# Attention and GLA decoder layer on one core: scalings with an accumulator, the inputs' low part one unit later, gate splits behind exponentials and copies, and the first rows squared first at the joint

## The chip, the cores and the metric

The kernel runs on one core of a Trainium2 chip. Its engines are called here as in the profile: PE (TensorE, products and transposes), DVE (VectorE), ACT (ScalarE), POOL (GpSimd) and SP (SyncE, which here only starts transfers). Each engine works through its own queue in order; semaphores make one wait for another. The time is device microseconds for one execution, lower being better. Three runs of the kernel before took 2201.93, 2202.55 and 2204.05 us.

## The reference

One layer of a decoder whose heads are split in two groups, on 2048 prompt tokens and 8 x 8 sample tokens. The core of it:

```python
def hybrid_layer(x, pos, ...):
    h = rms_norm(x, g_mix_pre)
    proj = jnp.einsum('btd,de->bte', h, w_in)
    q, k, v, gq, gk, gv, gr, glr = jnp.split(proj, points, axis=-1)
    q, k = rope(q), rope(k)
    attn = swa_banded(q, k, v, sinks)            # window of 128, 8 heads, 2 kv heads, sinks
    log_a = log_sigmoid(glr @ w_gk2 + b_gk) / 16
    o, s_new = gla_chunked(gq, gk, gv, log_a, s0)    # 4 heads, gated linear attention
    o = rms_norm(o, g_gla) * silu(gr)
    x = x + rms_norm(concat(attn, o) @ w_out, g_mix_post)
    h = rms_norm(x, g_ffn_pre)
    u = relu(h @ w_up)
    return x + rms_norm((u * u) @ w_down, g_ffn_post), ...

def sink_softmax(scores, mask, sink):
    m = max(max(scores), sink)
    p = exp(scores - m)
    return p / (sum(p) + exp(sink - m))
```

All of it is fp32. The model's width is 1024, the inner width of the MLP 4096. The keys, values and states that go to the next step are outputs too.

## The kernel before

**Numbers.** Products on PE take operands in a rounded form (fp32r). So most operands are split into a high part (ACT copies and rounds) and a low part (DVE subtracts the high part from the source), and a product is made of three: high-high, high-low and low-high. In names, h and l end the two parts: xh, xl for the transposed inputs, ph, pl for the transposed probabilities, qh, ql, kh, kl for queries and keys. The gate's weights wg are split in the same way, after a multiply by the gain of the norm (gcol).

**Attention stage** (about 30 to 305 us). The prompt is cut into 16 blocks of 128 tokens. For each block i the loop runs four units u = 0 to 3, one for two heads each. A unit (function `unit`) is a generator of steps: scores sc on PE; mask and maximum on DVE (a custom reduction that writes s and m); exponentials on ACT, with their sum den; reciprocal and scaling of s by it (line 501 on DVE, 499 on ACT for one of eight scalings in half of the units); transposes pT on PE; ph on ACT; pl on DVE; products av on PE, first ph with the values, then pl; and the sum mo. Three units are in work at a time (ahead, now, behind). Around their steps the loop puts the work for other blocks: projections of block i + 2 fill PE, and a table, `A_PLAN`, says in which unit and phase (T, A, X, S, B, C in this order) each piece of the rest is issued: x0 and x1, the low parts of the two halves of the transposed inputs of block i + 3; klo and lo, low parts of keys and queries; rstd, the norm's power on POOL. The queues follow this order of issue.

Every result of PE goes to a bank of PSUM. The kinds d and e, with the transposed inputs xT and the av products, have one buffer each, the others two.

From block 3 on, two pieces of the gate's weights are fetched per block (16 pieces of 128 x 384 in the stage, 192 KB each, into two buffers). `split_gw` multiplies a piece by gcol on POOL (line 261), copies the high part on ACT and subtracts on POOL (263). `A_SPLIT` says that two pieces are split at phase B of unit 0. The first two pieces are split in block 4. `split_gained` (221) does the same work for later pieces without the multiply: ACT copies with a scale, and DVE multiplies and subtracts in one instruction.

SP starts the loads and stores, in order: the pieces' loads, the stores of mixed rows, and the stores of each block's transposed inputs (xt_d, 512 KB for each part).

**GLA stage** (about 300 to 700 us). For each block, level products are put into one matrix AH by predicated copies (`put_level`), copied to AT, and the state S is updated (1179); then PE makes o. The sample's output goes through `finish_out` with i == NB, in the midst of a prompt block's work: norm over each head (squares on ACT, power on POOL giving ors), then four scalings on DVE (1088), and after two pauses of 44 products their transposes on PE.

**Joint** (about 700 to 890 us). Output projections of 128 rows each, `out_projecting`, in the order `B_ORDER`. While one set of rows is projected, `residual` works on earlier ones: norm, residual sum, second norm, scaling by its gain (1515), transposes to PE (xnT, 1525), and splits. The first rows come with their sum made already; of them only the second norm is left. The second rows are the ones called bx.

Of the kernel before, what the change touches and what calls it, by code (L numbers as in the profile page):

```python
# [16 lines left out]
ALU = mybir.AluOpType  # L17
# [4 lines left out]
P = 128  # L22
# [3 lines left out]
NB = T // P  # L26
# [27 lines left out]
H_EARLY, H_LATE = (1, 2), (5, 7, 6, 3, 4)  # L54
G_EARLY, G_LATE = (0, 1), (2, 3)
A_FILL = ((11, 2, 0), (10, 0, 2), (10, 0, 0), (12, 1, 0))
A_LEAD, A_SPLIT = 14, (2, 1, 0, 0)
A_PLAN = [(name, (int(at[0]), at[1])) for name, at in dict(
    klo0="3T", first="1B", hi1="3C", x1="1B", lo1="0A", klo1="0B", x0="0C", rest="3A", lo0="3A", junk="2A", turn="1A", rstd="1A", vl="3S"
).items()]  # L60
G_FIRST = (0, 1)
G_NEXT = (NB, *range(2, NB))
G_ORDER = (0, 1, 2, 3)
G_FILL = (34, 14, 16, 8, 20)
# [76 lines left out]
def hybrid_step_kernel(ctx: ExitStack, tc: tile.TileContext, I, O):  # L141
# [113 lines left out]
        return c, k, load_raw(sp, k, G_AT + c * G_N, G_N, f"wg{c}", *stage)  # L255

    def split_gw(c, k, raw):
        if c in G_LATE:
            split_gained(gw[c][1][:, k, :], gw[c][2][:, k, :], raw, k)
            return  # L260
        nc.gpsimd.tensor_tensor(raw, raw, gcol[:, k : k + 1].to_broadcast([P, G_N]), op=ALU.mult)
        ac.activation(gw[c][1][:, k, :], raw, AF.Copy)
        nc.gpsimd.tensor_tensor(gw[c][2][:, k, :], raw, f32(gw[c][1][:, k, :]), op=ALU.subtract)
# [201 lines left out]
    def unit(i, r, jj, mo):  # L465
# [31 lines left out]
        for u in range(2):  # L497
            if u == 0 and r == jj:
                ac.activation(s[:, u, :nk], s[:, u, :nk], AF.Copy, scale=den[:, u : u + 1])
            else:  # L500
                dv.tensor_scalar(s[:, u, :nk], s[:, u, :nk], den[:, u : u + 1], None, op0=ALU.mult)
        yield
        pT = bank([P, nkt, 2, P], "c", f"pT_{u_}")
        for u in range(2):
# [289 lines left out]
    for i in range(NB):  # L794
# [29 lines left out]

        def do(u, phase):
            for name, at in A_PLAN:
                if at == (u, phase) and name in todo:
                    todo.pop(name)()

        for u in range(4):  # L830
            next(now)
            do(u, "T")
            next(behind, None)
            next(now)
            do(u, "A")
            later = next(queue)
            next(later)
            run(fill, A_FILL[u][0])
            next(behind, None)
            if u != 3:  # L840
                next(behind, None)
            run(fill, A_FILL[u][1])
            if u == 0:
                next(now)
            if u < 2 and new:
                hi, todo[f"x{u}"] = x_half(i + 3, u)
                hi()
            elif u == 2:
                todo.update(heads_T(i + 1))
            do(u, "X")  # L850
            run(fill, A_FILL[u][2])
            if u:
                next(now)
            do(u, "S")
            if u == 3:
                next(behind, None)
            next(behind, None)
            next(ahead)
            next(now)
            do(u, "B")  # L860
            split_some(A_SPLIT[u] if i < NB - 1 else 1)
            next(now)
            do(u, "C")
            behind, now, ahead = now, ahead, later
# [210 lines left out]
    def finish_out(i, og_src, sg, n, kind):  # L1075
# [9 lines left out]
            yield 44, True  # L1085
        og = next(ogs) if i < NB else gp_s[:, :512].rearrange("p (h d) -> p h d", h=4)
        for h in range(4):
            nc.vector.scalar_tensor_tensor(
                og[:n, h, :], og_src(h), rs[:n, h : h + 1], sg[:n, h * P : (h + 1) * P],
                op0=ALU.mult, op1=ALU.mult,  # L1090
            )
        for _ in range(S_WAIT[0] if i == NB else 1):
            yield 44, True
        pt = bank([P, 4, P], kind, f"ogT_{i}")
# [519 lines left out]
    for n, i in enumerate(B_ORDER[2:]):  # L1614
# [1 line left out]
        mixing = out_projecting(nc.tensor, i, early[-1][1])  # L1616
        run(mixing, 24 if i == B_ORDER[-1] else 48)
        if n == 0:
            second = residual(*early.pop(1))
            next(second)  # L1620
            next(second)
        elif n == 1:
            run(second)
        if i == B_ORDER[-1]:
            waiting_rows = residual(*early.pop(0))
            run(waiting_rows, 5)
        elif n != 1:
            run(residual(*early.pop(0)))
        run(mixing)
        if n == len(B_ORDER) - 5:  # L1630
# [614 lines left out]
```

## Time and profile before

| | |
|---|---|
| median of three runs | 2202.55 us (2201.93 to 2204.05) |
| the profiled execution | 2200.13 us |
| span of its trace, first to last instruction | 2198.2 us |
| mean granted clock of TensorE | 0.997 |
| attention stage, 36.7 to 300 us: PE / DVE / ACT / POOL busy | 255.98 / 227.65 / 223.00 / 152.64 us |
| GLA, 300 to 700 us: PE / DVE / ACT busy | 396.4 / 299.0 / 250.5 us |
| joint, 700 to 890 us: PE / DVE / ACT busy | 188.32 / 120.31 / 82.89 us |
| MLP, 890 to 2198 us: PE / DVE / ACT busy | 1290.11 / 866.61 / 643.28 us |

Busy times are those of the trace's windows. In a row of the timeline the first number is the start and the second the duration, in us; the words behind name engine, line, operation, what is written and read, and the shape; "x2" joins equal instructions in a row. In square brackets stands how long the engine sat idle before, and who released it. DVE's and ACT's rows overlap their neighbours at both ends, so the step from one start to the next is shorter than a duration. Most of the small instructions carry line 130, that of a helper that records them; they are told apart by the names of their tiles.

### The profile page before, as it was taken

The numbers are of one execution on the slowest core, as the hardware profiler recorded it, in microseconds if no ns is written. First come the engines' busy times: TensorE is split into PE (matmuls) and PEld (weight loads), VectorE is DVE, ScalarE is ACT, GpSimd is POOL, SyncE is SP. The second block draws the span as 40 slices with busy tenths as digits, with TensorE's granted clock in tenths as the row PEclk, the third lists the DMA queues.
The fourth block names the chain that finished last, engine by engine and source line by source line (L and its number), as shares of the span: only waits on it lengthen the run. The fifth ranks groups of instructions, "written<-read, shape, count | busy, mean of one in ns | idle before, by whom it ended". The sixth has DMA issues, their size and how long they took to land.

```text
span 2198.2 us, 34114 instructions
## 1 busy us (share of the span) xinstructions
PE 2158.6 (98%) x11784; PEld 1861.8 (85%) x11784; DVE 1532.1 (70%) x3101; ACT 1220.7 (56%) x2626; POOL 261.8 (12%) x418
## 2 busy tenths in 40 slices
PE   8999999999999999899999999999999999999998
PEld 7989989999998888788888887888888888888886
DVE  5888868777786665888888655548676666555566
ACT  5889867556664443555555544435454544444454
POOL 3576512121211100000000000000000000000000
PEclk9999999999999999999999999999999999999999
DMA  7344232214436765868777676758554433766685
GB/s 229 131 137 157 97 103 73 68 63 145 142 126 230 224 204 185 277 219 278 269 254 260 236 237 220 241 181 268 182 187 158 138 138 146 239 201 193 195 271 185
DMA packets 240314, 411.53 MB, mean 187 GB/s; under 512 B 25925, under 2 KB 142125, under 8 KB 236029
## 3 DMA queue, kind: packets, MB, share of 16 engines
q1 hardware_dynamic: 240140, 409.35, 56.1%
q8 instruction: 93, 1.52, 0.3%
q14 instruction: 81, 0.66, 0.1%
HBM read 265.82 MB, written 143.99 MB: 186 GB/s over the span
## 4 chain that ended last, share of the span: by engine, by line
PE 85%; DVE 6%; ACT 4%; DMA 3%; issue 1%; POOL 1%; SPq 0%; DVEq 0%; ACTq 0%; POOLq 0%
PE dn L130 26%; PE gproj L130 10%; PE uc L130 8%; PE uX L130 7%; PE out L1318 6%; PE proj L130 5%; PE ue L130 4%; PE ud L130 4%; PE ub L130 4%; PE sam L130 1%; PE dsam L130 1%; PE av L130 1%; PE o L130 1%; PE pT L130 1%; PE sc L130 1%
## 5 line engine op out<-in xcount | busy, mean ns | idle before, releaser
L130 PE MATMUL dn<-o0t,o0s 128*128 128x512 f32 x896 | 349.2, 390 | 2.5 <-ACT f L2013 1.6
L130 PE MATMUL dn<-o1t,o0s 128*128 128x512 f32 x896 | 349.5, 390 | 0.5 <-DVE o1t L219 0.4
L130 PE MATMUL dn<-o0t,o1s 128*128 128x512 f32 x896 | 349.3, 390 | 0.0
L219 DVE TENSOR_TENSOR o1s<-rs,o0s 128x512 fp32r<-128x512 f32 x224 | 154.8, 692 | 229.8 <-ACT o0s L218 226.1
L218 ACT ACTIVATE o0s<-rs 128x512 fp32r<-128x512 f32 x224 | 141.1, 631 | 305.9 <-PE dn L130 286.8
L130 PE MATMUL gproj<-wg,gxh 128*128 128x384 f32 x1024 | 272.5, 342 | 0.3 <-DVE gp_s L213 0.3
L130 PEld LDWEIGHTS dn<-o0t,o0s 128*128 128x128 f32 x896 | 168.2, 188 | 39.5 <-ACT f L2013 2.0
L130 PEld LDWEIGHTS dn<-o1t,o0s 128*128 128x128 f32 x896 | 168.2, 188 | 37.6 <-DVE o1t L219 1.6
L130 PEld LDWEIGHTS dn<-o0t,o1s 128*128 128x128 f32 x896 | 168.2, 188 | 35.4
L130 ACT ACTIVATE st<-st 128x512 f32<-128x512 f32 x224 | 141.2, 630 | 99.9 <-DVE st L130 94.8
L130 PE MATMUL uc<-H,s 128*128 128x512 f32 x768 | 188.1, 394 | 2.8 <-ACT st L130 2.8
L130 PEld LDWEIGHTS gproj<-wg,gxh 128*128 128x128 f32 x1024 | 183.8, 188 | 4.1 <-issue 3.1
L130 PE MATMUL gproj<-wg,gxl 128*128 128x384 f32 x576 | 186.0, 340 | 0.3 <-DVE gp_s L213 0.3
L130 PE MATMUL uX<-H,w 128*128 128x512 f32 x768 | 185.2, 390 | 0.0
L130 PEld LDWEIGHTS uc<-H,s 128*128 128x128 f32 x768 | 144.2, 189 | 33.7 <-ACT st L130 3.0
L130 PEld LDWEIGHTS uX<-H,w 128*128 128x128 f32 x768 | 144.0, 188 | 30.3
L219 DVE TENSOR_TENSOR o1t<-rt,o0t 128x512 fp32r<-128x512 f32 x224 | 153.3, 685 | 9.5 <-ACT o0t L218 9.4
L1318 PE MATMUL out<-wo,mt 128*128 128x512 f32 x680 | 158.6, 392 | 0.0
L208 POOL TENSOR_TENSOR frs<-rs_v,half 128x1 f32<-128x1 f32 (+1 forms) x13 | 10.1, 785 | 1209.9 <-DVE rs_v L206 689.6
L1318 PEld LDWEIGHTS out<-wo,mt 128*128 128x128 f32 x680 | 126.5, 188 | 26.1
L218 ACT ACTIVATE o0t<-rt 128x512 fp32r<-128x512 f32 x224 | 138.3, 618 | 10.4 <-DMA rt<-t_d 6.2
L130 DVE TENSOR_TENSOR st<-st 128x512 f32<-128x512 f32 x160 | 110.7, 692 | 28.7 <-ACT st L130 24.5
(404 smaller groups left out, 4302.1 us busy)
## 6 DMA issues: line engine op xcount, KB each, us to landing
s_d<-st SPq DMA_DIRECT2D x32, 1792.0 KB, 8.4
rs<-s_d SPq DMA_DIRECT2D x224, 256.0 KB, 2.8
raw<-in_w_up SPq DMA_DIRECT2D x64, 512.0 KB, 4.9
rt<-t_d SPq DMA_DIRECT2D x128, 256.0 KB, 3.8
rt<-in_w_down SPq DMA_DIRECT2D x96, 256.0 KB, 3.1
t<-in_w_down SPq DMA_DIRECT2D x64, 256.0 KB, 3.9
t_d<-t SPq DMA_DIRECT2D x32, 512.0 KB, 3.3
hraw<-h_d SPq DMA_DIRECT2D x20, 512.0 KB, 5.4
```

The lines of the kernel that those rows point to most:

```text
L130: ins = call(*a, **k)
L208: nc.gpsimd.tensor_tensor(out, v[:n], e, op=ALU.pow)
L218: nc.scalar.activation(hi, src, AF.Copy)
L219: vector.tensor_tensor(lo, src, f32(hi), op=ALU.subtract)
L1318: te.matmul(banks[c], x, w[:, c * 512 : (c + 1) * 512], start=k + u == 0, stop=k == KT - 1 and u == len(products) - 1,)
```

## The change

Five edits, and no change of what is computed.

1. The 96 scalings of s on DVE get a second operation, an addition of 0.0, and an accumulator output into m, which nothing reads afterwards.
2. x0 moves from phase C of unit 0 to phase A of unit 1, but for block 0. So DVE subtracts the first half's low part behind the reduction and the pl that came after it.
3. The two pieces of a block's gate weights are split one at a time, in unit 1: one at phase A (on ACT behind the exponentials), one at phase B (behind copies). The last block is as it was. Pieces (0, 2) and (0, 3), those split in block 4, go through `split_gained`.
4. The sample's four scalings in `finish_out` are issued behind the copy of AT instead of between the level copies.
5. At the joint, the square of the first rows is issued ahead of the work on the second ones, and their transposes come 13 products sooner on PE.

```diff
-A_LEAD, A_SPLIT = 14, (2, 1, 0, 0)
+A_LEAD = 14
 A_PLAN = [(name, (int(at[0]), at[1])) for name, at in dict(
-    klo0="3T", first="1B", hi1="3C", x1="1B", lo1="0A", klo1="0B", x0="0C", rest="3A", lo0="3A", junk="2A", turn="1A", rstd="1A", vl="3S"
+    klo0="3T", first="1B", hi1="3C", x1="1B", lo1="0A", klo1="0B", rest="3A", lo0="3A", junk="2A", turn="1A", rstd="1A", vl="3S", x0="1A"
 ).items()]
+G_GAINED = ((0, 2), (0, 3))
...
     def split_gw(c, k, raw):
-        if c in G_LATE:
+        if c in G_LATE or (c, k) in G_GAINED:
             split_gained(gw[c][1][:, k, :], gw[c][2][:, k, :], raw, k)
             return
...
-                dv.tensor_scalar(s[:, u, :nk], s[:, u, :nk], den[:, u : u + 1], None, op0=ALU.mult)
+                dv.tensor_scalar(
+                    s[:, u, :nk], s[:, u, :nk], den[:, u : u + 1], 0.0, op0=ALU.mult, op1=ALU.add,
+                    accum_out=m[:, u : u + 1],
+                )
...
             for name, at in A_PLAN:
+                if name == "x0" and i == 0:
+                    at = 0, "C"
...
             do(u, "A")
+            if u == 1 and i < NB - 1:
+                split_some(1)
...
             do(u, "B")
-            split_some(A_SPLIT[u] if i < NB - 1 else 1)
+            if u == 1 or i == NB - 1:
+                split_some(1)
...
         for h in range(4):
-            nc.vector.scalar_tensor_tensor(
-                og[:n, h, :], og_src(h), rs[:n, h : h + 1], sg[:n, h * P : (h + 1) * P],
-                op0=ALU.mult, op1=ALU.mult,
-            )
+            with tc.issue_after(put[0].ins) if i == NB else nullcontext():
+                nc.vector.scalar_tensor_tensor(
+                    og[:n, h, :], og_src(h), rs[:n, h : h + 1], sg[:n, h * P : (h + 1) * P],
+                    op0=ALU.mult, op1=ALU.mult,
+                )
...
         if n == 0:
-            second = residual(*early.pop(1))
+            first_rows = residual(*early.pop(0))
+            next(first_rows)
+            second = residual(*early.pop(0))
             next(second)
             next(second)
+            run(first_rows)
...
-        elif n != 1:
+        elif n > 1:
             run(residual(*early.pop(0)))
```

**Where instructions move.** The first place is DVE's queue at the start of block 4, before and then changed. ISA is the masking reduction and its read of the accumulator; the numbers in the names are unit (of s, pT, pl) or half (of xT).

```order
L130 TENSOR_TENSOR kl_1458<-pk_1453,kh_1457 64x128
L130 TENSOR_TENSOR xl_1618<-xT_0_1619,xh_1617 128x512
L130 ISA s_0_1_1497,m_0_1_1648<-sc_0_1_1626,amask,sink 128x256
L130 ISA m_0_1_1648 128x1
L130 ISA s_0_1_1497,m_0_1_1648<-sc_0_1_1626,amask,sink 128x256
L130 ISA m_0_1_1648 128x1
L130 TENSOR_TENSOR pl_0_0_1645<-pT_0_0_1631,ph_0_0_1644 128x512
L130 TENSOR_SCALAR rs_v<-ssq_1425 128x1
L130 RECIPROCAL den_0_1_1652<-den_0_1_1652 128x2
L130 TENSOR_SCALAR s_0_1_1497<-s_0_1_1497,den_0_1_1652 128x256 x2
```

```order
L131 TENSOR_TENSOR kl_1458<-pk_1453,kh_1457 64x128
L131 ISA s_0_1_1497,m_0_1_1641<-sc_0_1_1626,amask,sink 128x256
L131 ISA m_0_1_1641 128x1
L131 ISA s_0_1_1497,m_0_1_1641<-sc_0_1_1626,amask,sink 128x256
L131 ISA m_0_1_1641 128x1
L131 TENSOR_TENSOR pl_0_0_1639<-pT_0_0_1631,ph_0_0_1638 128x512
L131 TENSOR_SCALAR rs_v<-ssq_1425 128x1
L131 TENSOR_TENSOR xl_1618<-xT_0_1619,xh_1617 128x512
L131 SCALAR_TENSOR_TENSOR wg_1_191<-wg_raw_1543,gcol,wg_0_190 128x384
L131 RECIPROCAL den_0_1_1645<-den_0_1_1645 128x2
L131 TENSOR_SCALAR s_0_1_1497,m_0_1_1641<-s_0_1_1497,den_0_1_1645 128x256 x2
```

The low part xl of half 0 has gone from ahead of the reductions and pl to behind them, and in this block a gate weight's low part (wg_1) follows it. In the other blocks the wg row is not there. ACT's queue at the same place:

```order
L130 ACTIVATE xh_1617<-xT_0_1619 128x512
L130 ACTIVATE wg_0_190<-wg_raw_1543 128x384
L130 ACTIVATE wg_0_190<-wg_raw_1545 128x384
L130 ACTIVATE ph_0_0_1644<-pT_0_0_1631 128x512
L130 ACTIVATE s_0_1_1497,den_0_1_1652<-s_0_1_1497,m_0_1_1648 128x257 x2
L130 ACTIVATE rest_0_0_1682<-av_0_0_1677 64x256
```

```order
L131 ACTIVATE xh_1617<-xT_0_1619 128x512
L131 ACTIVATE ph_0_0_1638<-pT_0_0_1631 128x512
L131 ACTIVATE s_0_1_1497,den_0_1_1645<-s_0_1_1497,m_0_1_1641 128x257 x2
L131 ACTIVATE wg_0_190<-wg_raw_1543,gcol 128x384
L131 ACTIVATE rest_0_0_1678<-av_0_0_1673 64x256
L131 ACTIVATE xh_1617<-xT_1_1680 128x512
L131 ACTIVATE qk_1702<-proj_0_1439,rstd_all 128x392
L131 ACTIVATE wg_0_190<-wg_raw_1545,gcol 128x384
```

The copies of the weights have moved behind ph and the exponentials, and the second one behind qk.

The second place is SP's queue in an ordinary block with two pieces (block 6), before and changed:

```order
L231 DMA wg_raw_2100<-in_w_in 128x384
L231 DMA wg_raw_2102<-in_w_in 128x384
L323 DMA xt_d_89<-xh_1879 128x1024
L323 DMA xt_d_89<-xl_1880 128x1024
L285 DMA x_2096<-in_x_prompt 128x1024
```

```order
L232 DMA wg_raw_2098<-in_w_in 128x384
L324 DMA xt_d_89<-xh_1877 128x1024
L232 DMA wg_raw_2100<-in_w_in 128x384
L324 DMA xt_d_89<-xl_1878 128x1024
L286 DMA x_2094<-in_x_prompt 128x1024
```

The second piece's load stands behind a store of the high part, and the low part's store and the next inputs' load stand behind it. On POOL the multiplies of these two loads stay ahead of the casts of kh and kl.

The third place is ACT's queue at the joint, before and changed; bx are the second rows, mt_9446 or mt_9444 the first ones, out the banks of the second rows' projection.

```order
L1412 ACTIVATE bjunk_9607,bssq_9606<-out_0_9241 128x512
L1412 ACTIVATE bjunk_9607,bssq_9606<-out_1_9465 128x512
L1512 ACTIVATE bjunk_9607,bssq_9606<-bx_9554 128x1024
L1512 ACTIVATE bjunk_9621,bssq_9620<-mt_9446 128x1024
L1601 ACTIVATE w_0_0_10699<-raw_0_0_10693 128x1024
```

```order
L1522 ACTIVATE bjunk_9605,bssq_9604<-mt_9444 128x1024
L1422 ACTIVATE bjunk_9609,bssq_9608<-out_0_9239 128x512
L1422 ACTIVATE bjunk_9609,bssq_9608<-out_1_9463 128x512
L1544 ACTIVATE ht_9545<-xnT_0_9626 128x512
L1522 ACTIVATE bjunk_9609,bssq_9608<-bx_9552 128x1024
```

The first rows' square has gone from behind the second rows' two norms to ahead of both, and the copy of the first rows' transposes (ht) now stands ahead of the square of bx. On PE the eight transposes of the first rows follow 4 instead of 17 products of the rows that are then in work.

## The prediction

> **What bounds the kernel now.** I read the page's busy times first.
>
> ```profile
> PE 2158.6 (98%) x11784; PEld 1861.8 (85%) x11784; DVE 1532.1 (70%) x3101; ACT 1220.7 (56%) x2626; POOL 261.8 (12%) x418
> ```
>
> TensorE (PE) is busy for 2158.6 of the span's 2198.2 us, and the change takes no product from it. So all that can be won is idle time of PE, 39.6 us in all. The view of the waits says who ends that time; the columns are total us, times, longest:
>
> ```profile
> PE av L130 <- DVE rs_v L130: 2.4, 11, 0.3
> PE av L130 <- ACT ph L130: 1.8, 1, 1.8
> PE xnT L1525 <- DVE x L1515: 1.7, 1, 1.7
> PE sc L130 <- POOL kl L450: 1.4, 1, 1.4
> PE pT L130 <- DVE s L130: 1.0, 1, 1.0
> ```
>
> The edits lie beside four of these rows and one more in the GLA stage; only the wait on kl is not aimed at. Next I read windows that run from one block's first av product to the next one's: block 4, then an ordinary block.
>
> ```profile
> core 0: us, PE busy (x) PEld busy (x) DVE busy (x) ACT busy (x) POOL busy (x), PEclk, DMA share, GB/s
> 94.06:112.42 18.36, 16.32 (x110) 15.13 (x109) 14.45 (x44) 14.55 (x41) 12.07 (x22) 1.00 0.37 129
> 145.47:161.89 16.42, 16.19 (x111) 15.34 (x110) 15.08 (x44) 14.77 (x42) 11.78 (x21) 1.00 0.41 141
> ```
>
> In an ordinary block PE is idle for 0.23 of 16.42 us, while VectorE (DVE) is busy for 92% and ScalarE (ACT) for 90% of it. Little can be won per block, and two engines are nearly full. Block 4 lasts 1.94 us longer.
>
> **The low part moved (x0).** An ordinary block in the timeline, PE's rows and then DVE's:
>
> ```profile
> 145.47 0.28 PE L130 MATMUL av<-ph,vv 128*128 128x256 f32 x1
> 145.97 0.45 PE L130 MATMUL av<-pl,vv 128*64 128x256 f32 x2 [0.23 <-DVE rs_v L130]
> 149.89 0.28 PE L130 MATMUL av<-ph,vv 128*128 128x256 f32 x1
> 150.01 0.39 PE L130 MATMUL av<-pl,vv 128*64 128x256 f32 x2
> ```
>
> ```profile
> 143.82 0.69 DVE L130 TENSOR_TENSOR xl<-xT,xh 128x512 fp32r<-128x512 f32 x1
> 144.43 0.47 DVE L130 CUSTOM_DVE_ANT_0 s<-sc,amask,sink 128x256 f32<-128x256 f32 x1
> 144.82 0.08 DVE L130 DVE_READ_ACCUMULATOR2_ANT m<- 128x1 f32 x1
> 145.23 0.69 DVE L130 TENSOR_TENSOR pl<-pT,ph 128x512 fp32r<-128x512 f32 x1
> 146.33 0.81 DVE L130 TENSOR_SCALAR s<-s,den 128x256 f32<-128x256 f32 x2
> ```
>
> The second av product follows the first by 0.12 us where nothing is late (149.89 to 150.01); at the block's start it takes 0.50, so 0.38 us are lost. The releaser is named rs_v, but what the product reads is pl, which ends at 145.92 because xl stands ahead of it. With xl behind pl, DVE's chain to pl is shorter by xl's step, 143.82 to 144.43, so 0.61 us, and pl is ready at about 145.3, before PE asks. That stall goes.
>
> What is late next: xl's reading frees the bank of the transposed inputs, and this kind of bank has one buffer. xl will run from about 145.3 to 146.0, and PE, 0.38 us earlier than now, wants the bank for the second half's xT at about 146.0. I give 0.13 back: 0.25 us gained per block. Bounds: 0.38 (the bank is just free) and 0 (xl is held up 0.25 more). The wait is there 11 times, in ten ordinary blocks and in block 4.
>
> Queued behind the moved xl are the reciprocal and two scalings, and behind these PE's transposes of s. The scalings start at 146.33 now and at about 146.4 then; PE asks for them 1.1 us after it asks for xT. This holds if a pair takes no longer than its 0.81 us now.
>
> **The accumulators.** Six of eight scalings in a block, 96 in all. By tile (shortest, median, longest in ns), and one slow pair beside GpSimd (POOL):
>
> ```profile
> L130 DVE CUSTOM_DVE_ANT_0 s<-sc,amask,sink x128: 341/480/485, 37.6 to 298.9; 128x256 f32<-128x256 f32 x120, 128x128 f32<-128x128 f32 x8
> L130 DVE TENSOR_SCALAR s<-s,den x96: 280/354/885, 39.2 to 300.4; 128x256 f32<-128x256 f32 x90, 128x128 f32<-128x128 f32 x6
> 150.10 1.08 DVE L130 TENSOR_SCALAR s<-s,den 128x256 f32<-128x256 f32 x2
> 149.95 0.83 POOL L261 TENSOR_TENSOR wg_raw<-wg_raw,gcol 128x384 f32<-128x384 f32 x1 [0.35 <-DMA wg_raw<-in_w_in]
> ```
>
> A scaling takes 354 ns in the median and up to 885, and the long ones stand beside POOL's work, as the pair at 150.10 beside the multiply at 149.95. The form with an accumulator has no row. Its nearest is the reduction with an accumulator over the same shape: 480 ns with no such spread, a step of 0.40 us (144.43 to 144.82 and the next). Bounds for one scaling: 0.354 us (nothing changes but the waits) and 0.56 (480 plus a read of 0.08 that overlaps nothing). I take a step of 0.40, by the nearest row. The two pairs shown take 0.81 and 1.08 us, so a block's six cost about 3 x 0.95 = 2.8 us of DVE now; six steps make 2.4. That is DVE's time, off PE's path wherever PE does not wait for s, and it does so once, for 1.0 us in the first blocks, where POOL is busiest. There I take 0.4 us; bounds 0 and 1.0.
>
> [...]
>
> **Gate splits.** In block 4, where the first two pieces meet:
>
> ```profile
> 109.73 1.60 POOL L261 TENSOR_TENSOR wg_raw<-wg_raw,gcol 128x384 f32<-128x384 f32 x2
> 110.58 0.52 ACT L130 ACTIVATE wg<-wg_raw 128x384 fp32r<-128x384 f32 x1 [2.03 <-POOL wg_raw L261]
> 112.42 0.38 PE L130 MATMUL av<-ph,vv 128*128 128x256 f32 x1 [1.82 <-ACT ph L130]
> ```
>
> ACT stands 2.03 us for the multiply, the copy ph is queued behind it, and PE stands 1.82 us for ph. The two pieces concerned will have no multiply, and their copies stand behind the exponentials and behind the copy of qk. So the 1.82 goes, and the block's av gap with it (0.25 to 0.38). Against that stand two new DVE rows of 128x384, some 0.5 us each (0.69 for 512 elements, the row of xl); the first is ahead of the scalings and costs about 0.2. Together 1.9; bounds 1.2 and 2.1.
>
> In blocks 5 to 10 the second piece of the two comes late instead. Its buffer is free only when POOL has subtracted, at about 149.2 in the block shown, by my count of POOL's queue, and its load then needs the median:
>
> ```profile
> wg_raw<-in_w_in SPq DMA_DIRECT2D x32, 192.0 KB, 2.7
> 152.23 0.63 POOL L440 CAST kh<-kh 64x128 fp32r<-64x128 f32 x2 [1.26 <-ACT kh L130]
> 153.51 0.29 POOL L450 CAST kl<-kl 64x128 fp32r<-64x128 f32 x1
> 154.80 0.28 PE L130 MATMUL sc<-kl,qh 128*128 128x256 f32 x1
> ```
>
> It lands at 151.9 and its multiply (0.83) ends at 152.75, ahead of the casts that start at 152.23 today. These slide by 0.52, and kl ends at 154.32; PE asks for it at 154.55, 0.25 sooner than now. The margin is 0.2 us, so I take 0.05 lost in each of these six. Behind the casts on POOL nothing else is due for PE. Gains: blocks 2, 3, 11 and 12 at 0.25 make 1.0; six at 0.2 make 1.2. For the last blocks, where POOL has little to block with and the scalings only get longer, I take off 0.3. The stage: 1.0 + 1.2 + 1.9 + 0.4 - 0.3 = 4.2.
>
> **The sample's output (GLA).**
>
> ```profile
> 477.02 0.34 DVE L1088 SCALAR_TENSOR_TENSOR gp_s<-s_ob,ors,s_sg 64x128 f32<-64x128 f32 x1 [1.11 <-POOL ors L208]
> 480.72 0.49 PE L130 MATMUL o<-gp,AT 128*128 128x128 f32 x2 [0.74 <-DVE S L1179]
> ```
>
> Today the level copies that make AT wait behind this scaling, 1.11 us for POOL's ors, and have three more scalings between them. Without these four the copy of AT comes 1.11 + 0.34 us sooner or more, and PE's 0.74 goes. The scalings then run behind S, and their reader on PE stands behind two pauses of 44 products: hidden. 0.8 with the product's start-up; bounds 0.5 and 0.9.
>
> **The joint.**
>
> ```profile
> 709.22 15.02 PE L1318 MATMUL out<-wo,mt 128*128 128x512 f32 x65
> 710.98 0.50 SPq L1422 DMA_DIRECT2D mt<-x_first  x1
> x_d<-x_first SPq DMA_DIRECT2D x1, 512.0 KB, 4.2
> 721.31 1.06 ACT L1512 ACTIVATE bjunk<-bx 128x1024 bf16<-128x1024 f32 x1 [6.76 <-DVE bx L1420]
> 722.49 1.06 ACT L1512 ACTIVATE bjunk<-mt 128x1024 bf16<-128x1024 f32 x1
> 724.48 1.28 DVE L1515 SCALAR_TENSOR_TENSOR x<-mt,bssq,gpre 128x1024 f32<-128x1024 f32 x1 [0.59 <-POOL bssq L208]
> 725.91 1.06 PE L1525 MATMUL xnT<-ident,x 128*128 128x128 f32 x8 [1.68 <-DVE x L1515]
> ```
>
> The first rows' square (mt, 722.49) stands on ACT behind the second rows' (bx), which idles 6.76 us for its input. The first rows are issued at 710.98; with the 4.2 us of the store beside them they are in place by about 715.2. Squared then, with both halves of the second rows' squares, POOL's powers and the second rows' scalings ahead, they are scaled at 720.0 to 721.4. PE now asks for them 13 products sooner: 724.23 - 13 x 0.231 = 721.2 (15.02 / 65 = 0.231). So they are ready, or 0.2 late; the 1.68 goes, and some of the start-up: 1.75 (bounds 1.0 and 1.8). The second rows are scaled later, and PE reads them a group of 48 products further on.
>
> **Sum.** 4.2 + 0.8 + 1.75 = 6.75, rounded up to 7.1 for PE's start-up after the pauses that go: the span falls from 2198.2 to 2191.1. The profiled execution took 2200.13; the median of the runs, 2202.55, lies 2.4 above it, and I set the loss against the median: 2202.55 - 7.1 = 2195.4 us.
>
> **The rivals.** 0.2%, here 4.4 us, is about what a measurement of this kernel can tell from no change.
>
> *The stall only moves* (0.22). The bank's wait eats x0's gain, longer scalings eat the first blocks', and kl the rest. Block 4, GLA and joint remain at their lower bounds, 1.2 + 0.5 + 1.0 = 2.7, or at 1.9 + 0.8 + 1.75 = 4.4 at the most: about 2199. For it: DVE at 92%. Against: the chain to pl is 0.61 shorter whatever follows.
>
> *Every stall goes* (0.10). 10 x 0.38 + 2.1 + 1.0 + 0.9 + 1.8 = 9.6, with start-up 11: 2191.5. For it: PE's idle time, 39.6 us, is four times that. Against: the single bank.
>
> *The second piece lands late* (0.12): slower than before. SP issues that load behind a store of 512 KB. If it lands 2 us after 151.9, POOL's multiply holds the casts and PE stands 1.8 us at the scores, in six blocks 10.8. With 1.2 of gain there gone as well, the balance is 10.8 - 5.9 = +4.9: 2207. It decides from about 1.2 us of lateness on. For it: the store ahead, and POOL's fixed queue. Against: the DMA share of the block is 0.41.
>
> **How the numbers follow.** The forecast has 0.56 and runs from 2192.5 to 2198. The range, 2190.5 to 2202, takes in the first two rivals and leaves out the slower case and a little at both ends. Faster by more than 0.2% (below 2198.15): 0.56 + 0.10, less 0.01 for overlap, 0.65; within: 0.22 and 0.01, 0.23; slower: 0.12.
>
> **What would show it.** In the changed profile: no wait of av for rs_v or pl at the blocks' starts; block 4's window near 16.5 us, ordinary ones near 16.2; scalings between 0.35 and 0.5 us with no long ones; no wait of xnT at the joint, none of o for S at the sample. Wrong would be waits of xT for xl, of sc for kl in blocks 5 to 10, or of pT for s in many blocks.

## The result and the profile after

The changed kernel takes 2193.86 us in the median of six runs (2190.8 to 2195.49), the kernel before 2202.24 in six (2200.37 to 2204.05). The ratio is 0.9966, with a 95% interval of 0.9955 to 0.9977, so about 8 us were won, give or take 2.4. The profiled execution took 2193.01 with a span of 2191.2, 7.0 below the span before. Forecast were 2195.4 and a span of 2191.1.

PE's waits in the changed kernel (us in total, times, longest):

```profile
PE sc L131 <- POOL kl L451: 4.0, 4, 1.4
PE av L131 <- DVE pl L131: 1.8, 3, 1.1
PE xnT L131 <- ACT ht L131: 1.0, 1, 1.0
PE pT L131 <- DVE s L131: 0.6, 1, 0.6
PE o L131 <- DVE S L1189: 0.6, 1, 0.6
```

The row of av for rs_v (2.4 in 11 places) is gone, the 1.8 of av for ph is gone, xnT no longer waits for x at the joint, and o waits for S once instead of twice. The wait of pT for s has fallen from 1.0 to 0.6, that of av for pl has grown from 0.9 to 1.8. And the wait of the scores for kl has grown from 1.4 in one place to 4.0 in four. The windows from one block's first av product to the next one's show where. They are named here by the block whose av begins them: 3 (the window that the prediction calls block 4, since block 4's late av ends it), 6, 7 and 11.

```profile
core 0: us, PE busy (x) PEld busy (x) DVE busy (x) ACT busy (x) POOL busy (x), PEclk, DMA share, GB/s
93.56:109.51 15.95, 15.95 (x110) 15.52 (x110) 14.50 (x50) 14.61 (x41) 10.11 (x19) 1.00 0.43 149
142.58:159.44 16.86, 16.07 (x111) 15.58 (x110) 14.62 (x50) 14.61 (x41) 11.76 (x21) 1.00 0.43 138
159.44:176.41 16.97, 16.06 (x110) 15.58 (x110) 14.60 (x50) 14.60 (x41) 11.75 (x21) 1.00 0.40 136
225.44:241.30 15.86, 15.86 (x111) 15.52 (x110) 14.50 (x50) 13.90 (x38) 8.09 (x17) 1.00 0.27 101
```

Window 3 is down from 18.36 us. Without pieces of the gate's weights on the way (the last row) a block takes 15.86 in place of 16.39, and PE never idles. With two pieces, blocks 6 and 7 take 16.9 in place of 16.4: here the change makes the kernel slower. One of them in detail, SP's queue, POOL's and PE's:

```profile
161.36 0.38 SPq L324 DMA_DIRECT2D xt_d<-xh  x1
163.24 0.79 SPq L232 DMA_DIRECT2D wg_raw<-in_w_in  x1
```

```profile
162.20 1.01 POOL L264 TENSOR_TENSOR wg<-wg_raw,wg 128x384 fp32r<-128x384 f32 x1
165.33 0.83 POOL L262 TENSOR_TENSOR wg_raw<-wg_raw,gcol 128x384 f32<-128x384 f32 x1 [2.12 <-DMA wg_raw<-in_w_in]
167.05 0.83 POOL L262 TENSOR_TENSOR wg_raw<-wg_raw,gcol 128x384 f32<-128x384 f32 x1 [0.90 <-DMA wg_raw<-in_w_in]
167.94 0.64 POOL L441 CAST kh<-kh 64x128 fp32r<-64x128 f32 x2
169.24 0.29 POOL L451 CAST kl<-kl 64x128 fp32r<-64x128 f32 x1
```

```profile
169.58 0.39 PE L131 MATMUL sc<-kl,qh 128*128 128x256 f32 x1 [0.91 <-POOL kl L451]
```

POOL frees the second piece's buffer at 163.21, SP starts the load at 163.24, it lands at 167.05, POOL multiplies till 167.88, and only then come the casts of kh and kl. PE stands 0.91 us for kl. This is the prediction's third rival, at a lateness below its 2 us.

The scalings are now another instruction, with a read behind it (shortest, median, longest in ns):

```profile
L131 DVE TENSOR_SCALAR_CACHE_REDUCE s<-s,den x96: 344/478/483, 39.2 to 297.5; 128x256 f32<-128x256 f32 x90, 128x128 f32<-128x128 f32 x6
L131 DVE DVE_READ_ACCUMULATOR s<-s,den x96: 80/82/85, 39.5 to 297.9; 128x1 f32 x96
```

The spread up to 885 is gone, the median is up from 354. The sum is nearly the same: for the 128x256 ones a mean of 483 before and 479 now. In the first blocks, where the prediction looked for their gain, PE's two rows before and then changed are:

```profile
54.46 0.33 PE L130 MATMUL pT<-ident,s 128*128 128x128 f32 x1 [1.03 <-DVE s L130]
57.56 0.33 PE L130 MATMUL av<-pl,vv 128*64 128x256 f32 x1 [0.70 <-DVE pl L130]
```

```profile
54.37 0.33 PE L131 MATMUL pT<-ident,s 128*128 128x128 f32 x1 [0.62 <-DVE s L131]
57.90 0.33 PE L131 MATMUL av<-pl,vv 128*64 128x256 f32 x1 [1.11 <-DVE pl L131]
```

The 0.41 us won at s come back as 0.41 more at pl; the block from 44 us on takes 17.6 us in both kernels.

The joint, with rows of ACT, DVE and PE:

```profile
709.96 1.06 ACT L1522 ACTIVATE bjunk<-mt 128x1024 bf16<-128x1024 f32 x1 [0.42 <-DMA mt<-x_first]
714.84 1.27 DVE L1525 SCALAR_TENSOR_TENSOR x<-mt,bssq,gpre 128x1024 f32<-128x1024 f32 x1
717.10 1.03 PE L1535 MATMUL xnT<-ident,x 128*128 128x128 f32 x8
```

The scaled rows are there at 716.1, 1.0 us before PE asks.

**Where the 7 us went.** PE runs the same products in the same order but for the eight transposes at the joint, so each product's start can be compared between two traces. PE is ahead of the kernel before by 2.9 us at the last av product (304.65 before, 301.76 after), and by 4.0 at the last o of the GLA stage (701.90, 697.87): 1.1 more, 1.0 of it at the sample. It is 5.9 ahead behind the joint's transposes, 1.9 more. Near 890 us come another 1.4, with a wait for a store (xnT for ht, 2.3 before, 1.0 after), and the MLP gives 0.3 back. The first av product of all starts 0.3 us later in the changed kernel than before (44.25 and 43.93), which is scatter (the table's section has four profiles of one stage between 43.80 and 44.71); from that product on the attention stage is 3.2 us shorter.

### The profile page after: what moved, and what is told of

The parts are those of the page before. It is cut to its first block, busy times and chain, and to the rows that moved or that the text cites. A ratio compares the mean times of both kernels' runs of the same rounds, so it can differ in the third digit from the quotient of the medians.

```text
span 2191.2 us, 34210 instructions
## 1 busy us (share of the span) xinstructions
PE 2156.9 (98%) x11784; PEld 1864.8 (85%) x11784; DVE 1530.7 (70%) x3199; ACT 1219.1 (56%) x2626; POOL 257.7 (12%) x414
## 4 chain that ended last, share of the span: by engine, by line
PE 89%; ACT 3%; DVE 3%; DMA 2%; POOL 1%; issue 1%; SPq 0%; DVEq 0%; POOLq 0%; ACTq 0%
PE dn L131 27%; PE gproj L131 11%; PE uc L131 8%; PE uX L131 7%; PE out L1328 7%; PE proj L131 5%; PE ud L131 4%; PE ub L131 4%; PE ue L131 4%; PE sam L131 1%; PE dsam L131 1%; PE o L131 1%; PE sc L131 1%; PE out L131 1%; PE av L131 1%; PE pT L131 1%
```

## The experiments

Twelve kernels ran. The table gives, from each profile, the time from one block's first av product to the next in a block with two pieces (6) and in one without (11), the start of the attention stage's last av product, and the ratio of times to the kernel before with its interval. "Changed" means all five edits but for what the row says.

| kernel | block 6 | block 11 | last av | ratio |
|---|---|---|---|---|
| before | 16.42 | 16.39 | 304.65 | 1 |
| changed | 16.85 | 15.85 | 301.76 | 0.9966 (0.9955 to 0.9977) |
| changed, second profile | 16.67 | 15.85 | 300.88 | 0.9967 (0.9954 to 0.9980) |
| before + accumulators | 16.02 | 16.01 | 302.22 | 0.9982 (0.9973 to 0.9992) |
| before + x0 | 16.49 | 16.17 | 304.98 | 1.0009 (1.0000 to 1.0018) |
| changed, plain scalings | 17.14 | 16.16 | 306.43 | 0.9991 (0.9980 to 1.0002) |
| changed, x0 as before | 16.59 | 16.03 | 304.52 | 0.9968 (0.9955 to 0.9981) |
| changed, splits as before | 16.25 | 15.85 | 303.54 | 0.9974 (0.9962 to 0.9985) |
| the same, first two without multiply | 16.25 | 15.87 | 301.25 | 0.9964 (0.9950 to 0.9978) |
| changed, second pieces off POOL | 16.77 | 15.89 | 304.13 | 0.9977 (0.9967 to 0.9986) |
| changed, joint as before | 16.81 | 15.85 | 300.88 | 0.9978 (0.9968 to 0.9987) |
| changed, sample's scalings as before | 16.80 | 15.85 | 301.77 | 0.9972 (0.9960 to 0.9983) |
| changed, both pieces in phase A | 15.89 | 15.86 | 298.69 | 0.9954 (0.9940 to 0.9968) |
| changed, pieces in 0B and 1A | 15.85 | 15.86 | 298.38 | 0.9955 (0.9942 to 0.9968) |

The two profiles of the changed kernel agree within 0.9 us at the last av product. The kernels with the joint or the sample's scalings as before have the same attention stage, so they make four profiles of it: 300.88 to 301.77. Two things part them: the first av product starts between 43.80 and 44.71 in the four, and blocks 6 to 8, with the waits for kl, take between 16.58 and 16.97 us each. A difference below 1 us in this column shows nothing. Times alone tell two kernels apart from about 0.0025 of the ratio on, 5.5 us, so the verdicts below rest on the traces.

**The changed kernel with plain scalings.**

```diff
-                dv.tensor_scalar(
-                    s[:, u, :nk], s[:, u, :nk], den[:, u : u + 1], 0.0, op0=ALU.mult, op1=ALU.add,
-                    accum_out=m[:, u : u + 1],
-                )
+                dv.tensor_scalar(s[:, u, :nk], s[:, u, :nk], den[:, u : u + 1], None, op0=ALU.mult)
```

> The changed kernel without the accumulators on the 96 scalings. Theory: scalings are back at 354 ns in the median with up to 900 beside POOL, their mean about the same as with an accumulator (479), so the span is within 1 us of 2191.2, the wait of pT for s in block 1 back at 1.0 from 0.6. Rival (POOL is freed by the accumulators): POOL's instructions take longer, kl comes later still, and the waits of sc for kl grow by 0.2 to 0.5 in each of blocks 5 to 9: 1 to 3 us longer. Second rival (the accumulating form's length costs): 1 to 3 us shorter.

None of the three. The attention stage is 4.7 us longer than the changed kernel's, longer even than before, and whether the other edits alone gain anything is in doubt (0.9980 to 1.0002). The kl waits did not grow (2.7 in 4 places). DVE's and POOL's rows at the start of block 6 show what did:

```profile
144.92 1.33 DVE L131 TENSOR_SCALAR s<-s,den 128x256 f32<-128x256 f32 x2
157.75 1.23 DVE L131 TENSOR_SCALAR s<-s,den 128x256 f32<-128x256 f32 x1
```

```profile
144.83 1.00 POOL L264 TENSOR_TENSOR wg<-wg_raw,wg 128x384 fp32r<-128x384 f32 x1
157.55 1.28 POOL L401 TENSOR_TENSOR rot<-qk,tb 128x512 f32<-128x512 f32 x1
```

In these rows a plain scaling that starts 0.1 to 0.2 us behind a POOL instruction stands until that one is done: the single one ended at 158.98, POOL's rotation at 158.83. The changed kernel's pair beside the same subtraction:

```profile
143.06 1.00 POOL L264 TENSOR_TENSOR wg<-wg_raw,wg 128x384 fp32r<-128x384 f32 x1
143.08 0.48 DVE L131 TENSOR_SCALAR_CACHE_REDUCE s<-s,den 128x256 f32<-128x256 f32 x1
143.48 0.47 DVE L131 TENSOR_SCALAR_CACHE_REDUCE s<-s,den 128x256 f32<-128x256 f32 x1
```

Both scalings start while POOL works, and take a step of 0.40 us each all the same. So the two forms differ beside POOL: the plain one took up to 1233 ns in this kernel, and none of the changed kernel's 96 accumulating ones took over 483 ns.

**The kernel before with the accumulators alone.** The edit is the reverse of the last one, in the kernel before.

> The kernel before with the accumulators alone. Theory (a plain scaling stands still while POOL works, an accumulating one does not; what counts is how much sooner the queue behind it moves): scalings 0.40 us from start to start, none long, block 1's wait of pT for s down by 0.3 to 0.5, the 11 waits of av at the blocks' starts shorter by 0.1 to 0.2 each since the scaling ahead of them no longer waits for POOL; attention stage shorter by 1.5 to 2.5 us, span about 2196. Rival (all of what the change without accumulators lost, 4.5 us, belongs to the accumulators by themselves): stage 4 to 5 us shorter. Second rival (they only pay where the splits have put POOL's subtraction beside the scalings): under 0.7 us.

An ordinary block lasts 16.02 us, 0.38 to 0.40 less, with pieces or without. The last av product comes 2.4 us sooner, and that in spite of a stretch at 112 to 117 us in which this execution's clock was granted at 0.67: the window that holds it (4) took 17.8 us, 1.1 more than before, where the others gain 0.4. The first av product came 0.6 us later too. With the 0.6 and the 1.5 for the clock the stage is some 4.5 us shorter, by estimate. So the first rival comes nearest, and the theory's 1.5 to 2.5 was too low. The product behind av still stands 0.31 apart at the blocks' starts (145.75 and 146.06): in block 6 PE wins 0.19 at this wait, 0.11 at the transposes pT behind a slowed scaling (155.57) and 0.06 at an av product (158.13), the last two too short to be listed as waits. DVE's rows in the kernel before, in the middle of a block and shortly before its end:

```profile
154.69 0.83 DVE L130 TENSOR_SCALAR s<-s,den 128x256 f32<-128x256 f32 x1
155.44 0.34 DVE L130 SCALAR_TENSOR_TENSOR vv<-proj,rstd_all,vv 128x128 fp32r<-128x128 f32 x1
...
158.86 0.55 DVE L130 TENSOR_SCALAR s<-s,den 128x256 f32<-128x256 f32 x1
159.44 0.42 DVE L130 TENSOR_TENSOR mo<-av,rest 64x256 f32<-64x256 f32 x1
```

And with the accumulators:

```profile
154.77 0.48 DVE L130 TENSOR_SCALAR_CACHE_REDUCE s<-s,den 128x256 f32<-128x256 f32 x1
155.18 0.08 DVE L130 DVE_READ_ACCUMULATOR s<-s,den 128x1 f32 x1
155.18 0.35 DVE L130 SCALAR_TENSOR_TENSOR vv<-proj,rstd_all,vv 128x128 fp32r<-128x128 f32 x1
```

From 153.77 to the pl at the next block's start, 161.63, DVE's rows in the kernel before show no idle time at all. So what a scaling loses in this stretch arrives at that pl. The first of the two, beside POOL's rotary product (154.50 to 155.4), steps by 0.75 us, with the accumulator by 0.41; the second steps by 0.58 and, in the other trace, 0.52. Together that is 0.40, about the block's gain. The scalings that got longer stand where DVE has idle time. Its busy time in a block without pieces is the same before (14.48) and now (14.52), so the busy share says nothing of this.

**The kernel before with x0 alone.**

```diff
-    ..., x0="0C", rest="3A", ..., vl="3S"
+    ..., rest="3A", ..., vl="3S", x0="1A"
 ...
+                if name == "x0" and i == 0:
+                    at = 0, "C"
```

> The kernel before with the first half's low part in phase A of unit 1 alone. Theory (the term as predicted): av no longer waits at the blocks' starts, 0.38 us won each, and 0.1 to 0.2 lost at xT, because the scalings still stand still beside POOL: stage shorter by 1.5 to 2.5 us. Rival (the plain scalings behind it eat it, xT and pT late): under 0.7 us.

The rival holds: the last av product is 0.3 us later than before. Without pieces the move is worth 0.22 us in block 11, near what the prediction gave it (0.25); with pieces it costs 0.07. There, the second av product wins 0.31 and xT loses 0.34:

```profile
145.34 0.69 DVE L130 TENSOR_TENSOR pl<-pT,ph 128x512 fp32r<-128x512 f32 x1 [0.20 <-ACT ph L130]
146.00 0.68 DVE L130 TENSOR_TENSOR xl<-xT,xh 128x512 fp32r<-128x512 f32 x1
```

```profile
146.83 0.63 PE L130 MATMUL xT<-ident,x 128*128 128x128 f32 x4 [0.18 <-DVE den L130]
```

pl now waits 0.20 for ph, which stands on ACT behind the two copies of weights. xl follows pl, and its reading ends at 146.68; PE waits for the bank that xl reads, though the view names den.

**The changed kernel with x0 as before** (`x0="0C"` in the table).

> The changed kernel with the first half's low part in phase C of unit 0 as before. Theory: the wait at the blocks' starts (av for pl or rs_v) comes back at 0.35 to 0.5 us in ten blocks: the span is longer by 3.5 to 4.5 us, about 2195. Rival (what removed that wait were the copies moved behind ph on ACT): no longer by more than 1 us.

The last av product is 2.8 us later, 0.6 of it already at the first one. From the first to the last it is 2.2 us more than in the changed kernel's first profile and 3.0 more than in its second. So with accumulators and the split pieces x0 is worth 2 to 3 us, less than the theory's 3.5, more than the rival's 1. In the blocks without pieces it is worth less than alone, 0.18 in block 11 (16.03 and 15.85), for the accumulators have already taken a part of the same wait; blocks 4, 5 and 9 lose about 0.4 each, and in blocks 6 to 8 the waits for kl, which differ between executions, hide it. In the times it does not show (0.9968).

**The changed kernel with the splits as before.**

```diff
-            if u == 1 and i < NB - 1:
-                split_some(1)
...
-            if u == 1 or i == NB - 1:
-                split_some(1)
+            split_some(A_SPLIT[u] if i < NB - 1 else 1)
```

> The changed kernel with the gate splits as before (two pieces at once in unit 0, with POOL's multiply; no gained pieces), all else as changed. Theory (the second piece's late load holds POOL's casts): PE's wait of sc for kl falls from 4.0 us in 4 places to 1.4 in 1; block 4's wait of av for ph, 1.8, comes back with some 0.3 beside it; span 2191.2 - 2.6 + 2.1, so about 2190 to 2191, and windows of blocks 5 to 9 shorter by up to 1.2 each. Rival (the two copies ahead of ph make pl late again, whatever DVE does): the kl waits go, but av waits 0.3 to 0.4 in each of blocks 5 to 10 and in the other blocks as well, some 3 us: about 2193.

> The changed kernel with both pieces split at once in unit 0 as before, but with the first two pieces without POOL's multiply as in the change. Theory: the kl waits fall to 1.4 in 1, and block 4 keeps its gain, since what it needed was no multiply ahead of the copy: about 2188.5, 2.5 under the changed kernel. Rival: the place of the copies, ahead of ph, counts: av waits come back in the blocks with pieces, and block 4 gains 1 us less: about 2191.

Both in part. kl's wait falls to 1.1 or 1.4 in one place, as the theory said. But blocks 5 to 10 then take 16.25, not 15.85. The wait that takes its place is not the rival's (av) but the bank's:

```profile
PE av L131 <- ACT ph L131: 1.6, 1, 1.6
PE xT L131 <- DVE den L131: 1.5, 8, 0.2
PE sc L131 <- POOL kl L451: 1.1, 1, 1.1
```

The cause is that of x0 alone: two copies ahead of ph. The first row is block 4's, back with POOL's multiply. Without the multiply it is 1.2 (named rs_v), and the stage ends 2.3 us sooner than with it. Not all of this is the multiply's. PE is 1.0 us ahead behind the wait (1.8 won at av, 0.8 of it lost at the next product), and some 1.3 more come from the clock, which was low right there in the execution with the multiply and not in the other (112 to 117 us, with the multiply):

```profile
112.00:117.00 5.00, 4.48 (x22) 4.12 (x22) 4.21 (x15) 3.02 (x9) 2.74 (x5) 0.70 0.74 248
```

The place of the copies is worth another 1.0 in windows 3 and 4 (without the multiply they take 33.85 us together, in the changed kernel 32.88). In the blocks behind them the new place costs as much as it gains or more: 0.4 won at xT in six of them, 1.0 to 1.1 lost at kl in three and 0.3 in two, 1.4 net against the changed kernel's first profile and 0.7 against its second. In all, the kernel with the copies ahead of ph and without the multiply (301.25) can't be told from the changed one (300.88 to 301.77).

**Second pieces split without POOL.**

```diff
-G_GAINED = ((0, 2), (0, 3))
+G_GAINED = ((0, 2), *((c, k) for c in (0, 1) for k in (1, 3, 5, 7)))
```

> The changed kernel with the second piece of each block split by ACT and DVE without POOL, in all blocks with two pieces (the first one only in block 4, as in the change). Theory (POOL's multiply of the second piece, late, holds the casts of kl): the waits of sc for kl fall from 4.0 us in 4 places to 1.4 in 1; a DVE instruction of 0.6 more per block costs up to 0.2 in each of six; stage shorter by 1.5 to 2.6, span about 2189. Rival (DVE becomes the bound): waits of pT for s or av for pl of 0.3 or more in six blocks, and no gain. Second rival (the wait on kl has another cause, ACT's kh): it stays at 4.0.

The first rival holds. kl's wait falls to 1.3 in one place, and another takes its place:

```profile
PE av L131 <- DVE pl L131: 5.6, 10, 1.1
```

```profile
143.90:160.68 16.78, 16.23 (x111) 15.49 (x110) 15.13 (x51) 14.84 (x41) 9.97 (x19) 1.00 0.42 138
```

DVE goes from 14.6 to 15.1 us of a block, the new row stands ahead of the next reductions and pl, and PE waits 0.56 us for pl at the second unit's av. The stage is 2.4 us longer. DVE can't take in this place what POOL is spared.

**Both pieces in phase A of unit 1, and one in 0B with one in 1A.**

```diff
             do(u, "A")
             if u == 1 and i < NB - 1:
-                split_some(1)
+                split_some(2)
...
-            if u == 1 or i == NB - 1:
+            if i == NB - 1:
                 split_some(1)
```

> The changed kernel with both pieces split in phase A of unit 1, behind the exponentials, instead of one there and one behind the copies. ACT has 0.27 us idle and some slack before the second half's xh there, POOL subtracts twice in a row and both loads are started ahead of the store. Theory (what costs the change 2.6 us is that the second piece's buffer is freed 1.3 to 2 us too late): the waits of sc for kl go from 4.0 us in 4 places to 1.4 in 1, no new wait over 0.2 in a block; attention stage shorter by 2 to 2.8 us, span about 2188.5, and 2 to 3 us under the changed kernel in this batch. Rival (the second copy delays rest and xh by 0.5, and with them mo, xl and the bank of xT): a new wait of 0.3 to 0.5 in each of six blocks, stage within 0.7 of the changed kernel.

> The changed kernel with the first piece split in phase B of unit 0, ahead of ph, and the second in phase A of unit 1. Theory: kl's waits go as with both in unit 1, but one copy of 0.5 us stands ahead of ph, and the wait of xT for its bank, 0.45 in blocks 5 to 10 where both copies stood there, comes back at half that: stage shorter by 1 to 2 us than the changed kernel's. Rival (one copy fits in there): as good as both in phase A of unit 1.

The second version keeps PE busy throughout blocks 5 to 10, here in 6 and 7:

```profile
142.80:158.65 15.85, 15.85 (x111) 15.52 (x111) 14.50 (x50) 14.62 (x41) 11.56 (x21) 1.00 0.43 146
158.65:174.50 15.85, 15.85 (x111) 15.53 (x110) 14.50 (x50) 14.60 (x41) 11.54 (x21) 1.00 0.43 146
```

The first takes 15.9 us in five of these six blocks and 16.58 in block 8. There the second piece still lands late (POOL waits for it until 181.22), though its load stands ahead of the store, and PE waits for kl:

```profile
183.74 0.38 PE L131 MATMUL sc<-kl,qh 128*128 128x256 f32 x1 [0.56 <-POOL kl L451]
```

The stage ends 3.1 and 3.4 us sooner than in the changed kernel's first profile, 2.2 and 2.5 sooner than in its second. For the first version the theory holds in size, though kl's waits are 1.9 in two places and not 1.4 in one, and though the span (2191.9) doesn't show the gain, for a reason given at the end. For the second it fell: one copy ahead of ph costs nothing in blocks 5 to 10. It costs in block 4, where av waits 0.7 (window 4 takes 17.55 us, 16.93 in the first version), so that in sum its rival, as good as both in 1A, is right. In the same batch the medians are 2192.7 and 2193.11 against 2195.03 of the changed kernel. Their intervals overlap; that these two versions are faster than the changed kernel is shown by the stage, not by the times.

**The changed kernel with the joint as before, with the sample's scalings as before, and once more.** The first two undo edits 5 and 4.

> The changed kernel with the joint as before. Theory: the wait of xnT for x at the joint is back at 1.7, and PE is 1.6 to 1.8 us later behind it than in the changed kernel; all ahead of it is as in the changed kernel. The wait of xnT for ht near 890 us, 2.3 before and 1.0 changed, does not belong to this edit and comes out at either value. Rival: it does belong to it and is back at 2.3, so that the joint edit is worth 3.2.

> The changed kernel with the sample's four scalings between the level copies as before. Theory: the wait of o for S at the sample is back at 0.7, PE 0.8 to 1.0 later from there on, all else as changed; the ratio is 0.0004 worse, which the times alone can't tell. Rival (what S waits for there is something else): the wait stays under 0.3.

> The changed kernel once more, for a second profile and times beside the other three. If the wait of xnT for ht near 890 us (1.0 in the first profile) is set by the landing of the store ahead of it and not by the code, it may differ by up to 1.4 us here; if it belongs to the joint edit, it stays at 0.6 to 1.1. The attention stage and the joint should agree with the first profile within 0.5 us, and the MLP's waits by 2 us or so.

At the joint PE falls 1.9 us back by the end of the transposes, with the old wait of xnT for x back at 1.7. At the sample o waits 0.7 again, and PE is 1.0 later. Both are near what the theories say (1.6 to 1.8, and 0.8 to 1.0). The old joint's wait is not the same in every execution: in the kernel before with x0 alone it is 2.8, since the load that the second rows need landed later (DVE stands 3.92 us for it there, 2.93 in the kernel before). The square of the second rows stood on ACT ahead of the first rows' one, so a late load for the second rows held back the first. In the changed kernel's order it stands behind.

The wait for ht near 890 was 2.2 with the old joint, which speaks for the rival. But it was 1.6 in the changed kernel's second profile and 2.4 with x0 as before, which has the changed joint. It ends when the store of ht lands, here in the changed kernel's first profile:

```profile
890.28 1.09 ACT L131 ACTIVATE ht<-xnT 128x512 f32<-128x512 f32 x2 [1.80 <-DMA h_d<-ht]
```

The wait varies, by 0.6 us between two executions of one kernel (1.0 and 1.6). With the changed joint the wait is 0.6 to 1.6 in nine profiles of ten and 2.4 in one, with the old joint 1.5 to 2.4 in four. Whether the joint edit has a part in it stays open.

## Why the prediction was right, and where it was not

The time, the sign, the span and the range came out. That the sum came out so close was luck: the accumulators' term was some 4 us too small, the term for the second piece's load some 3 us too small, and 1.4 us came from a wait that the sum did not hold.

- **What can be won is PE's idle time.** Right: PE's products are the same, and the gains are waits that went.
- **x0, 0.25 us a block.** Right in size without pieces (0.22 alone, 0.18 behind the accumulators). Wrong for the six blocks with two pieces: alone it is worth nothing there. The step that failed is "wants the bank for the second half's xT at about 146.0. I give 0.13 back": it took pl's start from DVE's queue alone and missed that ph, behind two copies on ACT, would be the next to hold it.
- **The accumulators, 0.4 us, "off PE's path wherever PE does not wait for s".** This is the step that failed most. Alone they are worth 0.38 us a block and some 4.5 in the stage (the estimate above); taking them from the changed kernel costs 4.7 to 5.5. In the first blocks, where the 0.4 was booked, they won nothing: 0.41 went from the wait for s to the next one, for pl, with the accumulators alone as well. That the long scalings stand beside POOL's work (up to 885 ns before, 1233 without the accumulators in the changed kernel) and the price of the new form (a step of 0.40, measured 0.40) were right. Wrong was to look for the gain only where PE waits for s. The cost of "a block's six" was counted as three pairs like the two shown; but two of the six stand singly, and these step by 0.75 and 0.58 us in place of 0.40. They stand in a stretch of DVE's queue that runs without a gap into the pl for which PE waits; the prediction quoted that wait and laid it to xl, the last of a queue that was late as a whole.
- **Block 4, 1.9.** Between the two traces, 2.6 are won at its first products and 1.1 given back in the next 10 us: 1.5, inside the bounds of 1.2 to 2.1. By undoing, it is 1.0 for the multiply and 1.0 for the copies' place.
- **The second piece's load, 0.05 in six blocks.** The mechanism was forecast to the instruction, as a part of the sum and as a rival, and was mis-sized. PE lost 1.0 to 1.1 us in three blocks and 0.3 in two in the first profile, 0.7 to 0.9 and 0.3 in the second: 3 to 4 us in all, where the sum had 0.3. The buffer came free at 163.21, 3.8 us behind the block's start, as counted (149.2 - 145.47 = 3.7), but the load took 3.8 us, not the median 2.7. So in the block shown it was 1.2 late, at the point from which the rival was said to decide; only the shorter lateness in the others and the larger gain elsewhere kept it from doing so.
- **The stage:** forecast 4.2, measured 2.9 and 3.8 in two profiles, or 3.2 and 4.0 from the first av product on. No run shows by itself the 0.3 taken off for longer scalings in the last blocks; between the two traces PE's lead falls by 0.2 us from block 13's first av product (260.39 before, 257.30 changed) to the last one (304.65 and 301.76).
- **The sample, 0.8:** measured 1.0, and 1.0 by undoing it, a little over its bound of 0.9. **The joint, 1.75:** 1.9, and 1.9 by undoing it, a little over its bound of 1.8; the scaled rows came 1.0 us ahead of PE's asking, inside the forecast of 1.2 ahead to 0.2 late.
- **What the sum did not hold:** 1.4 us near 890, a store's landing. The 0.35 added for PE's start-up has no row of its own in the result; a product behind a wait lasts some 0.1 us longer in the traces (sc from kl 0.39 behind its wait of 0.91, 0.28 in the kernel before where it did not wait).

The first rival (*the stall only moves*) happened too, in part and at all three of its places: the bank, kl and the first blocks. It did not decide, because the accumulators paid ten times their term elsewhere.

## What to carry to other kernels

When PE waits once a block for another engine, follow that engine's queue back to its last idle row: every instruction in the stretch counts, not the last one alone, and neither the wait's name nor the busy share tells which. A VectorE scaling whose duration spreads while GpSimd works (280 to 885 ns here) is worth a look there; here the form that also writes an accumulator, though longer in the median (478 ns, 354 for the plain one), took the spread out (344 to 483 ns). And when a copy is moved later, follow its buffer to the next load and to the queue in which that load's consumer stands: here one step earlier in the same loop won 2 to 3 us more. Before the difference of two profiles is put down to an edit, compare the granted clock over the same stretch: here some 1.3 of 2.3 us were the clock's.

## What the runs showed of the hardware

The accumulating scaling is two instructions in the profile, each there 96 times: the scaling of 478 ns in the median and a read of 82. In the rows shown the read starts before the scaling's end, and the next instruction starts with the read (154.77 for 0.48 us, then the read and vv both at 155.18, with the accumulators alone): steps of 0.40 us (143.08 to 143.48 in the changed kernel).

A good part of the scatter between executions is the granted clock in short stretches. The window 396 to 404 us in the changed kernel's first profile and in that of the kernel with accumulators alone:

```profile
396.00:404.00 8.00, 8.00 (x100) 7.16 (x100) 5.95 (x17) 2.33 (x8) 0.29 (x1) 1.00 0.43 135
```

```profile
396.00:404.00 8.00, 8.00 (x81) 7.23 (x81) 3.95 (x10) 2.00 (x7) 0.00 (x0) 0.57 0.38 132
```

The number ahead of the last two columns is the granted clock. At 0.57 in place of 1.00, PE is some 3 us later behind these 8 us (0.43 x 8.00 = 3.4, by estimate). A clock of 0.76 to 0.88 over the window 392 to 406 us is found in six of the fourteen profiles, in kernels of all kinds, the changed kernel's second profile among them and not its first; the other eight have 1.00. PE does not wait in that window in any of the fourteen (14.00 of 14.00 us busy), nor ahead of it in the kernel with accumulators alone (6.00 of 6.00 from 390 to 396 us, at a clock of 1.00), and what lowers the clock there stays open. Two other such stretches lie at a wait of PE: one at 114 us behind the 1.6 us for ph, in two of the four profiles with a wait of 1.6 to 1.8 there (0.67 and 0.70 over 112 to 117 us), and one at 726.5 us (0.50 for 3.3 us) at the joint's wait of 2.8 in the kernel before with x0 alone. The low clock at 396 us is why the version with both pieces in phase A has a span of 2191.9, though it had gained 3.1 us by then: its lead on the changed kernel's first profile falls from 3.1 to 0.1 us between 396 and 401 us. A span of a single execution can't be read to better than these 3 us here; the starts of the same product in two traces can, stretch by stretch.
